# Linear attention's level products one level behind their decays and tied behind projections, and both directions' keys transposed ahead of their products

## The chip, the cores and the metric

The kernel runs on one core of one Trainium2 chip. The metric is the device time of one execution in microseconds (us). The time of the kernel before is the median of three runs.

The core has five engines that work side by side, each through its own list of instructions in order: TensorE (PE, matrix products; PEld is its weight load), VectorE (DVE), ScalarE (ACT), GpSimd (POOL) and SyncE (SP, which issues most transfers). An instruction that waits holds back everything behind it on its own engine.

## What is computed

One inference step of a two-layer network over 640 tokens (512 latent, 128 context), width 1024, all in float32. The first layer has neighbourhood attention heads beside four heads of bidirectional gated linear attention. The second has grouped-query attention. Both layers end in a gated convolutional feed-forward block. The change concerns the gated linear attention alone:

```python
def gla_scan(q, k, v, g, s0):
    # S_t = diag(alpha_t) S_{t-1} + k_t^T v_t, o_t = q_t S_t, g = log alpha <= 0
    ...
    def step(s, inp):
        qc, kc, vc, gc = inp
        bcum = jnp.cumsum(gc.astype(jnp.float32), axis=2)
        o_inter = jnp.einsum('bhid,bhde->bhie', qc * jnp.exp(bcum).astype(qc.dtype), s)
        diff = bcum[:, :, :, None, :] - bcum[:, :, None, :, :]
        decay = jnp.exp(jnp.where(causal[:, :, None], diff, -jnp.inf)).astype(qc.dtype)
        att = jnp.einsum('bhid,bhjd,bhijd->bhij', qc, kc, decay)
        o = o_inter + jnp.einsum('bhij,bhje->bhie', att, vc)
        blast = bcum[:, :, -1:, :]
        k_dec = kc * jnp.exp(blast - bcum).astype(kc.dtype)
        s_new = (jnp.exp(blast[:, :, 0, :])[..., None].astype(s.dtype) * s
                 + jnp.einsum('bhjd,bhje->bhde', k_dec, vc)).astype(s.dtype)
        return s_new, o

def gla_bidir(q, k, v, g_f, g_b, s0_f, s0_b):
    o_f, s_f = gla_scan(q, k, v, g_f, s0_f)
    flip = lambda a: jnp.flip(a, axis=2)
    o_b, s_b = gla_scan(flip(q), flip(k), flip(v), flip(g_b), s0_b)
    return o_f + flip(o_b), s_f, s_b
```

## The kernel before, in words

The activations lie with channels on the 128 partitions and the 640 tokens along the free axis, in two halves of 320 (`HN`). A float32 matrix product is done as three products of rounded parts: the weight is split into `wh` (ScalarE, line 111) and `wl` (VectorE, or GpSimd every second time in this layer, line 112), the activation into `hh` and `hl`. `step` (line 149) issues the three matmuls of one k-step into `mm`; `tokens_major` (line 578) does the same with tokens on the partitions, into `tm`, and copies each finished tile of 128 tokens to `v` (ScalarE for even tiles, VectorE for odd ones, lines 598 to 601). Its tiles take turns in two PSUM banks, so a tile needs the copy of the tile two before it.

`layer0` works on the linear attention in two pairs of heads, m = 0 and 1, in the order of the table `ORDER`: scores of pair 0 (`a0`), states of pair 0 (`s0`), scores of pair 1 (`a1`), outputs of pair 0 (`o0`), then `s1` and `o1`.

- `gla_scores` (line 834) builds the attention of each 128-token tile from levels. `level(h)` gives the decayed keys `ea` and queries `eb` for blocks of h tokens: differences of the running sums `cum` on VectorE (lines 852, 853), exponentials on ScalarE (line 832), times the keys on GpSimd (line 858) and times the queries on VectorE (line 859). Each of the six levels 0, 1, 2, 4, 8, 16 then has 40 small products `lev` on TensorE (line 872); VectorE masks their result (line 877) and GpSimd adds it up (line 879). Levels 32 and 64 come last; their products `off`/`offx` (lines 894, 898) are copied to `att` by ScalarE and VectorE (lines 903 to 908).
- `gla_states` (line 914) transposes the decayed keys `kd` on TensorE (`kdt`, line 933), copies them to `kt` on ScalarE (line 935) and multiplies them with the values (`ds`, line 940), one direction after the other. VectorE updates the states `S` (lines 945, 946).
- `gla_out` (line 951) puts `att`, `S` and the decayed queries `qd` together (`go`).

Between these pieces other work is fed in by a `Fill` (line 239), a queue of generators: first the values' projection `g_vg`, then four gate projections `rg`, then the projection `g_va` of the neighbourhood heads' values, and after `q0` the query and key projections `qk`. `fill.some(n, m)` takes n of its steps (6 `tm` or 3 `mm` matmuls each) and m steps of a side list, the modulation vectors of later layers: two VectorE instructions per step and 256 KB of weights from SyncE (lines 313, 316). The rates are constants: `RLEV` 7 and `SLEV` 2 after each level, `ROFF` 12 and `SOFF` 4 before `off`, `RST` 8 after each direction in `gla_states`, `ROUT` 6.

The order on each engine is not the program's. The kernel is built with a planner that runs through the program by priorities on an estimated timeline and puts each engine's instructions in the order that results. `tc.high_priority` shifts priorities, and `tc.issue_after(ins)` makes the instructions of its block that are on the engine of `ins` stand behind `ins`:

```python
            with tc.issue_after(ins):
                return r0.out, norm.rstd((1,), NV[1])[0]
```

Of the kernel before, what the change touches and what calls it, by code (L numbers as in the profile page):

```python
# [30 lines left out]
def kernel(ctx: ExitStack, tc: tile.TileContext, a: dict, o: dict):  # L31
# [29 lines left out]
    def P1(name, tag="p1"):  # L61
        return ps1.tile([P, 512], F32, tag=tag, name=name, bufs=2 if tag == "p1" else 1)
# [85 lines left out]

    def step(ps, w, k, hh, hl, h, start, stop):
        whi, wlo = w(k)  # L150
        s = slice(h * HN, h * HN + HN)
        for (x, y, st, sp_) in ((wlo, hh, start, False), (whi, hl, False, False), (whi, hh, False, stop)):
            nc.tensor.matmul(ps, x, y[:, s], start=st, stop=sp_)  # L153
# [85 lines left out]
    class Fill:  # L239


        def __init__(self):
            self.queue, self.aside, self.owed, self.after = [], [], 0.0, None
# [7 lines left out]
        def some(self, n, m=0):  # L251
# [326 lines left out]
    def tokens_major(src, n, H, vs, tag, bufs=None, out=None):  # L578
# [5 lines left out]
        for c in range(n // 256):  # L584
            ws = [weights(src[c, q], 1024, 256) for q in range(2)]
            for t in range(5):
                ps = P1("tm", ("mm", "po")[t % 2])[:, 0:256]
                s = slice(128 * t, 128 * t + 128)
                for k in range(KD):
# [4 lines left out]
                    nc.tensor.matmul(ps, hh[:, s], whi, start=False, stop=(k == KD - 1))  # L594
# [239 lines left out]
    def gla_scores(m, k, q, FG, fill):  # L834
# [29 lines left out]
        for li, h in enumerate(LEVELS):  # L864
            A, B = (k, q) if h == 0 else level(h)
            ps = PS("lev")
            for t in range(5):
                for e in range(2):
                    pe = slice(64 * e, 64 * e + 64)
                    for j in range(4):  # L870
                        s = slice(128 * t + 32 * j, 128 * t + 32 * j + 32)
                        nc.tensor.matmul(ps[32 * j:32 * j + 32, e, 32 * t:32 * t + 32], A[pe, s], B[pe, s], start=True, stop=True)
# [15 lines left out]
        for width in (32, 64):  # L888
            for e, pe, t, dst in blocks:
                if width == 32:  # L890
                    for j in range(4):
                        b = j // 2
                        s = slice(128 * t + 32 * j, 128 * t + 32 * j + 32)
                        nc.tensor.matmul(dst[32 * j:32 * j + 32, 64 * b:64 * b + 64], A32[pe, s],
                                         B32[pe, 128 * t + 64 * b:128 * t + 64 * b + 64], start=True, stop=True)
                    continue
                for b in range(2):
                    nc.tensor.matmul(dst[64 * b:64 * b + 64, 64 - 64 * b:128 - 64 * b],
                                     A64[pe, 128 * t + 64 * b:128 * t + 64 * b + 64],
                                     B64[pe, 128 * t + 64 - 64 * b:128 * t + 128 - 64 * b], start=True, stop=True)  # L900
# [13 lines left out]
    def gla_states(m, k, FG, vg, S, fill):  # L914
# [14 lines left out]
        for d in range(2):  # L929
            tiles = (0, 1, 2, 4) if d == 0 else (3, 2, 1, 4)  # L930
            pt = P1("kdt")
            for i, t in enumerate(tiles):
                nc.tensor.transpose(pt[:, 128 * i:128 * i + 128], kd[d][:, 128 * t:128 * t + 128], ident)
            kt = T("kt", "v2", n=512)
            nc.scalar.copy(kt[:, 0:512], pt)
            ds = P1("ds")
            for i, t in enumerate(tiles):
                for e, pe in col_pairs():
                    h = 2 * m + e
                    nc.tensor.matmul(ds[pe, 128 * i:128 * i + 128], kt[:, 128 * i + 64 * e:128 * i + 64 * e + 64],  # L940
                                     vg[t][:, 128 * h:128 * h + 128], start=True, stop=True)
# [7 lines left out]
            fill.some(RST)  # L949
# [675 lines left out]
```

## Time and profile before

| what | value |
|---|---|
| time, median of 3 runs (lowest to highest) | 1727.22 us (1725.24 to 1729.24) |
| time of the profiled execution | 1725.67 us |
| its span, first to last instruction | 1723.9 us |
| mean granted TensorE clock, share of full | 0.975 |
| busy, share of the span: PE, DVE, ACT, POOL | 95%, 73%, 43%, 12% |
| DMA | 175.22 MB, mean 102 GB/s |

A busy share is the part of the span in which an engine executes something. It is a mean over stages with different limits, so a stage is read by the table of windows, which gives busy time per engine in a stretch, and by what each engine waited for in it. Times in rows count from the first instruction of the span. A releaser (`<-DVE eb L859`) is the instruction that ended a wait last.

### The profile page before, as it was taken

The page shows a single profiled execution, that of the slowest core. Times are in us where ns is not written, and L with a number is a line of the kernel's source. Part 1 is how long each engine was busy: PE and PEld are TensorE (multiplying, and loading weights), DVE is VectorE, ACT ScalarE, POOL GpSimd, SP SyncE. Part 2 cuts the span into 40 slices and gives each one's busy share as a digit, 9 for nine tenths or more (in the row PEclk, how much of TensorE's full clock was granted, in tenths as well). Part 3 has the DMA queues.
Part 4 walks back from the last instruction along what each step waited for, and adds up shares of the span by engine and source line. Part 5 has one row for each costly group of instructions (what it writes and reads, how often), then busy time and mean ns, then how long its engine had stood idle before and what let it go on. Part 6 is the DMA issues. An engine that isn't in the chain of part 4 may idle for free.

```text
span 1723.9 us, 33442 instructions
## 1 busy us (share of the span) xinstructions
PE 1633.0 (95%) x13142; PEld 1560.4 (91%) x13142; DVE 1255.2 (73%) x2767; ACT 741.9 (43%) x1681; POOL 205.5 (12%) x473
## 2 busy tenths in 40 slices
PE   7969698999999999999999999999999999999997
PEld 6868687879999999999998888888999999999997
DVE  5899944875899989996656987885776544663664
ACT  4443254453533323322335676775453322331342
POOL 2235441310200000000003310100100000000001
PEclk8999899999999999999998999999999999999999
DMA  8623323332254455454232200120222222222222
GB/s 318 210 88 134 102 81 106 91 93 98 84 167 160 147 164 185 153 151 132 70 120 82 76 21 14 43 63 24 76 74 75 73 74 74 75 76 83 73 68 69
DMA packets 68014, 175.22 MB, mean 102 GB/s; under 512 B 7920, under 2 KB 9744, under 8 KB 66832
## 3 DMA queue, kind: packets, MB, share of 16 engines
q1 hardware_dynamic: 67024, 171.48, 30.7%
q8 instruction: 103, 1.69, 0.4%
q0 software_dynamic: 832, 1.60, 0.3%
q14 instruction: 55, 0.45, 0.1%
HBM read 165.71 MB, written 7.34 MB: 100 GB/s over the span
## 4 chain that ended last, share of the span: by engine, by line
PE 78%; DVE 13%; DMA 3%; ACT 2%; issue 2%; SPq 1%; POOL 0%; ACTq 0%; DVEq 0%; POOLq 0%
PE mm L153 66%; PE gpo L1310 2%; DVE wa L316 2%; DVE junk L316 2%; PE gpt L1298 1%; DMA wa<-in_ada_wt_dram 1%; PE gs L1289 1%; DVE wl L112 1%; PE gs L1290 1%; DVE mx L1036 1%; PE napo L1102 1%; PE ss L410 1%; DVE eb L853 1%; DMA bias<-in_na_bias_dram 1%; DVE eb L859 1%
## 5 line engine op out<-in xcount | busy, mean ns | idle before, releaser
L153 PE MATMUL mm<-hh,wl 128*128 128x320 f32 x2080 | 651.0, 315 | 9.2 <-DVE wl L112 4.1
L153 PE MATMUL mm<-hl,wh 128*128 128x320 f32 x2080 | 647.7, 312 | 0.4 <-DVE hl L456 0.4
L153 PE MATMUL mm<-hh,wh 128*128 128x320 f32 x2080 | 641.3, 311 | 0.0
L111 ACT CAST wh<-ws 128x512 fp32r<-128x512 f32 x376 | 228.5, 614 | 435.3 <-PE mm L153 401.9
L153 PEld LDWEIGHTS mm<-hh,wl 128*128 128x128 f32 x2080 | 394.0, 190 | 19.2 <-issue 9.0
L153 PEld LDWEIGHTS mm<-hl,wh 128*128 128x128 f32 x2080 | 395.1, 190 | 2.7 <-DVE h L445 1.2
L153 PEld LDWEIGHTS mm<-hh,wh 128*128 128x128 f32 x2080 | 393.5, 190 | 0.6 <-issue 0.2
L112 DVE TENSOR_TENSOR wl<-ws,wh 128x512 fp32r<-128x512 f32 x348 | 239.1, 689 | 146.5 <-ACT wh L111 145.3
L153 PE MATMUL mm<-glo,wh 128*128 128x320 f32 x704 | 217.7, 310 | 0.0
L153 PE MATMUL mm<-ghi,wh 128*128 128x320 f32 x704 | 217.7, 310 | 0.0
L153 PE MATMUL mm<-ghi,wl 128*128 128x320 f32 x704 | 215.8, 310 | 0.0
L488 DVE SCALAR_TENSOR_TENSOR x<-mm,mod,x 128x192 f32<-128x192 f32 (+2 forms) x240 | 96.9, 435 | 88.9 <-PE mm L153 88.0
L153 PEld LDWEIGHTS mm<-ghi,wl 128*128 128x128 f32 x704 | 132.3, 189 | 1.3 <-issue 1.3
L153 PEld LDWEIGHTS mm<-glo,wh 128*128 128x128 f32 x704 | 133.0, 189 | 0.0
L153 PEld LDWEIGHTS mm<-ghi,wh 128*128 128x128 f32 x704 | 132.8, 189 | 0.1
L316 DVE SCALAR_TENSOR_TENSOR junk<-wa,sb 128x512 f32<-128x512 f32 x160 | 116.9, 734 | 6.7 <-DMA wa<-in_ada_wt_dram 6.4
L316 DVE SCALAR_TENSOR_TENSOR wa<-wa,sb 128x512 f32<-128x512 f32 x160 | 118.2, 745 | 0.3
L522 POOL MEMSET u<- 128x1 f32 x88 | 8.5, 98 | 761.1 <-DVE gate L515 426.6
L525 ACT COPY u<-mm 128x320 f32<-128x320 f32 x88 | 37.7, 431 | 87.8 <-PE mm L153 82.1
L592 PE MATMUL tm<-wl,hh 128*128 128x256 f32 x200 | 58.9, 300 | 7.4 <-ACT v L601 4.4
L1042 ACT ACTIVATE gp<-gs,mx,rq 128x640 f32<-128x640 f32 x64 | 57.0, 891 | 17.3 <-DVE mx L1038 11.6
L528 ACT COPY u<-mm 128x192 f32<-128x192 f32 x88 | 28.4, 323 | 79.8 <-PE mm L153 79.8
(302 smaller groups left out, 2432.5 us busy)
## 6 DMA issues: line engine op xcount, KB each, us to landing
ws<-in_wu_dram SPq DMA_DIRECT2D x88, 512.0 KB, 3.5
wa<-in_ada_wt_dram SPq DMA_DIRECT2D x160, 256.0 KB, 3.1
ws<-in_wd_dram SPq DMA_DIRECT2D x32, 448.0 KB, 3.8
aw<-in_ada_w_dram SPq DMA_DIRECT2D x8, 1024.0 KB, 14.2
ws<-in_w_ab_dram SPq DMA_DIRECT2D x16, 512.0 KB, 10.5
ws<-in_wd_dram SPq DMA_DIRECT2D x16, 512.0 KB, 3.6
x<-in_xT_dram SPq DMA_DIRECT2D x16, 320.0 KB, 4.5
ws<-in_w_gqa_dram SPq DMA_DIRECT2D x10, 512.0 KB, 3.5
```

The source lines that it names most:

```text
L111: nc.scalar.copy(hi, src)
L112: eng.tensor_tensor(lo, src, hi, ALU.subtract)
L153: nc.tensor.matmul(ps, x, y[:, s], start=st, stop=sp_)
L316: nc.vector.scalar_tensor_tensor(w if v else junk, w, 1.0, cs[v, j], ALU.mult, ALU.mult, accum_out=acc[:, k, v, j:j + 1])
L410: nc.tensor.matmul(ps[0:rows, c:c + 2], part[:, t], onesd, start=True, stop=True)
L488: nc.vector.scalar_tensor_tensor(x[:, b:e], ps[:, b - HN * h:e - HN * h], gate[:, v, m:m + 1], old[:, b:e], ALU.mult, ALU.add)
L525: nc.scalar.copy(u[:, 1:321], ps)
L528: nc.scalar.copy(u[:, 321:513], ps[:, 0:192])
L592: nc.tensor.matmul(ps, hh[:, s], wlo, start=(k == 0), stop=False)
L853: nc.vector.tensor_tensor(v(eb), sides(NT, h, 1), sides(g, f, 0), ALU.subtract)
L1042: nc.scalar.activation(dst, src, AF.Exp, bias=mx[:, i:i + 1], accum_out=sm[:, i:i + 1], **kw)
L1310: last = nc.tensor.matmul(po[64 * f:64 * f + 64, 0:128], vs[t][:, 64 * kv:64 * kv + 64], mates[f]["x"][:, 128 * t:128 * t + 128], start=(t ...
```

## The change

Four things are changed in the first layer.

1. In `gla_scores` the products of a level are issued after the decays of the next level, so products run one level behind. Level 16's products come after the decays of level 32, and a further `fill.some(RLEV)` of seven steps follows them.
2. The products of the levels and the `off` products are tied: on TensorE they stand behind the newest matmul that the filling queue had issued by then (`fill.behind()`).
3. In `gla_states` both directions' keys are transposed and copied before the first direction's products. Four steps of the queue (`RST / 2`) follow each transposition and four each direction's products, where eight had followed each direction.
4. The transposes and the states' products are tied in the same way.

```diff
     def step(ps, w, k, hh, hl, h, start, stop):
...
-            nc.tensor.matmul(ps, x, y[:, s], start=st, stop=sp_)
+            newest[0] = nc.tensor.matmul(ps, x, y[:, s], start=st, stop=sp_).ins
...
+        def behind(self):
+
+            tie = ExitStack()
+            if self.newest is not None:
+                tie.enter_context(tc.issue_after(self.newest))
+            return tie
...
                 else:
                     n -= 1
+                    self.newest = newest[0]
...
-        for li, h in enumerate(LEVELS):
-            A, B = (k, q) if h == 0 else level(h)
+        def products(li, A, B):
             ps = PS("lev")
-            for t in range(5):
...
+            with fill.behind():
+                for t in range(5):
...
+        ready = None
+        for li, h in enumerate(LEVELS):
+            sides = (li, k, q) if h == 0 else (li, *level(h))
+            if ready:
+                products(*ready)
+            ready = sides
             fill.some(RLEV, SLEV)
         A32, B32 = level(32)
+        products(*ready)
+        fill.some(RLEV)
         A64, B64 = level(64)
         fill.some(ROFF, SOFF)
...
-        for width in (32, 64):
+        with fill.behind():
+            for width in (32, 64):
...
-        for d in range(2):
-            tiles = (0, 1, 2, 4) if d == 0 else (3, 2, 1, 4)
+        order = [(0, 1, 2, 4), (3, 2, 1, 4)]
+        kts = []
+        for d, tiles in enumerate(order):
             pt = P1("kdt")
-            for i, t in enumerate(tiles):
-                nc.tensor.transpose(pt[:, 128 * i:128 * i + 128], kd[d][:, 128 * t:128 * t + 128], ident)
+            with fill.behind():
+                for i, t in enumerate(tiles):
+                    nc.tensor.transpose(pt[:, 128 * i:128 * i + 128], kd[d][:, 128 * t:128 * t + 128], ident)
             kt = T("kt", "v2", n=512)
             nc.scalar.copy(kt[:, 0:512], pt)
-            ds = P1("ds")
...
+            kts.append(kt)
+            fill.some(RST / 2)
+        for d, tiles in enumerate(order):
+            kt, ds = kts[d], P1("ds")
+            with fill.behind():
...
-            fill.some(RST)
+            fill.some(RST / 2)
```

The planner then orders every engine of this layer anew. Behind this layer the same kinds of work follow one another as before. Three places show what moved.

TensorE, where the `off` products of the second pair of heads begin. `tm` are matmuls of the value projection `g_va`, `mm` those of the next projection. Before:

```order
L593 MATMUL tm<-wh,hl 128x256
L594 MATMUL tm<-wh,hh 128x256
L894 MATMUL off<-eb,ea 32x64
L592 MATMUL tm<-wl,hh 128x256
L894 MATMUL off<-eb,ea 32x64
L593 MATMUL tm<-wh,hl 128x256
L894 MATMUL off<-eb,ea 32x64
L594 MATMUL tm<-wh,hh 128x256
L894 MATMUL off<-eb,ea 32x64
```

and now:

```order
L603 MATMUL tm<-wh,hl 128x256
L604 MATMUL tm<-wh,hh 128x256
L915 MATMUL off<-eb,ea 32x64 x16
L915 MATMUL offx<-eb,ea 32x64 x4
L915 MATMUL off<-eb,ea 32x64 x16
L915 MATMUL offx<-eb,ea 32x64 x4
L155 MATMUL mm<-hh,wl 128x320
L155 MATMUL mm<-hl,wh 128x320
L155 MATMUL mm<-hh,wh 128x320
```

Before, the products are strewn among the last `tm` matmuls: of the 480 `tm` of both value projections 54 stand behind the first `off` row, and 75 behind the sixth `lev` block of this pair. Now none stands behind the first `off` row, and 24 behind the sixth block.

ScalarE, where the keys of the first pair are copied (`kt`); `eb` and `ea` are exponentials of the second pair's levels. Before:

```order
L111 CAST wh<-ws 128x512
L935 COPY kt<-kdt 128x512
L679 COPY rg<-mm 128x320
L111 CAST wh<-ws 128x512
L832 ACTIVATE eb<-eb 128x640
L832 ACTIVATE ea<-ea 128x640
L832 ACTIVATE eb<-eb 128x640
L935 COPY kt<-kdt 128x512
L601 COPY v<-tm 128x256
```

and now:

```order
L842 ACTIVATE eb<-eb 128x640
L111 CAST wh<-ws 128x512
L689 COPY rg<-mm 128x320
L111 CAST wh<-ws 128x512
L958 COPY kt<-kdt 128x512 x2
L611 COPY v<-tm 128x256 x2
L842 ACTIVATE ea<-ea 128x640
L842 ACTIVATE eb<-eb 128x640
```

The second copy stood behind three exponentials and now stands beside the first, with one of them ahead.

VectorE, in the last levels of the second pair; `cum` rows are the differences, `eb<-eb,kqg` the multiplications by the queries, `acc` the masked products. Before:

```order
L877 TENSOR_TENSOR acc<-lev,mask_112 128x320
L852 TENSOR_TENSOR ea<-cum 128x640
L853 TENSOR_TENSOR eb<-cum 128x640
L112 TENSOR_TENSOR wl<-ws,wh 128x512
L877 TENSOR_TENSOR acc<-lev,mask_112 128x320
L852 TENSOR_TENSOR ea<-cum 128x640
L853 TENSOR_TENSOR eb<-cum 128x640
L859 TENSOR_TENSOR eb<-eb,kqg 128x640 x2
```

and now:

```order
L887 TENSOR_TENSOR acc<-lev,mask_112 128x320
L862 TENSOR_TENSOR ea<-cum 128x640
L863 TENSOR_TENSOR eb<-cum 128x640
L336 SCALAR_TENSOR_TENSOR A_5196<-mod_1987,normg 128x16
L869 TENSOR_TENSOR eb<-eb,kqg 128x640
L887 TENSOR_TENSOR acc<-lev,mask_112 128x320
L862 TENSOR_TENSOR ea<-cum 128x640
L863 TENSOR_TENSOR eb<-cum 128x640
L869 TENSOR_TENSOR eb<-eb,kqg 128x640
L609 COPY v<-tm 128x256
```

The same kinds of instructions follow one another. Up to the last multiplication of this pair there are 96 modulation instructions, 26 differences, 14 multiplications and 12 masks in both orders; a `wl` and a `v` copy that stood behind it now stand ahead of it.

## Rows read from the trace of the kernel before

**Rows 1.** The page: the span, and VectorE, TensorE and clock in 40 slices.

```profile
span 1723.9 us, 33442 instructions
...
PE   7969698999999999999999999999999999999997
...
DVE  5899944875899989996656987885776544663664
...
PEclk8999899999999999999998999999999999999999
```

**Rows 2.** Windows: us, busy PE, PEld, DVE, ACT, POOL, then PEclk, DMA share, GB/s.

```profile
80.00:120.00 40.00, 33.78 (x315) 31.18 (x314) 39.08 (x78) 21.57 (x39) 8.21 (x4) 0.96 0.37 125
120.00:160.00 40.00, 29.23 (x643) 26.94 (x641) 40.00 (x68) 11.76 (x21) 20.81 (x13) 0.87 0.33 115
160.00:200.00 40.00, 29.86 (x446) 27.67 (x443) 39.01 (x85) 14.00 (x32) 13.71 (x9) 0.87 0.33 112
200.00:219.00 19.00, 13.98 (x321) 13.29 (x319) 17.87 (x25) 7.08 (x12) 14.33 (x10) 0.82 0.23 75
219.00:240.00 21.00, 21.00 (x247) 18.85 (x248) 4.56 (x11) 9.59 (x24) 8.27 (x7) 1.00 0.33 108
```

**Rows 3.** TensorE's waits from 96 to 231 us: total, times, longest.

```profile
PE lev L872 <- DVE eb L859: 8.6, 4, 5.0
PE ds L940 <- ACT kt L935: 7.2, 1, 7.2
...
PE mm L153 <- DVE wl L112: 4.1, 1, 4.1
PE tm L592 <- DVE v L599: 2.3, 1, 2.3
PE lev L872 <- DVE acc L877: 2.3, 1, 2.3
...
PE off L894 <- DVE eb L859: 1.4, 1, 1.4
```

**Rows 4.** VectorE's groups by form, 96 to 231 us: busy, mean ns, idle before.

```profile
L316 DVE SCALAR_TENSOR_TENSOR wa<-wa,sb 128x512 f32<-128x512 f32 x27 | 25.7, 964 | 0.1
L316 DVE SCALAR_TENSOR_TENSOR junk<-wa,sb 128x512 f32<-128x512 f32 x27 | 25.0, 935 | 0.8 <-DMA wa<-in_ada_wt_dram 0.7
L859 DVE TENSOR_TENSOR eb<-eb,kqg 128x640 f32<-128x640 f32 x14 | 17.5, 1268 | 0.5 <-ACT eb L832 0.5
```

**Rows 5.** ScalarE's and TensorE's timelines at the second key copy: start, us, instruction, idle before.

```profile
180.96 0.74 ACT L832 ACTIVATE eb<-eb 128x640 f32<-128x640 f32 x1 [9.94 <-DVE eb L853]
...
183.07 0.57 ACT L935 COPY kt<-kdt 128x512 f32<-128x512 f32 x1
...
183.69 1.97 PE L940 MATMUL ds<-v,kt 128*64 128x128 f32 x16 [7.18 <-ACT kt L935]
```

**Rows 6.** VectorE's timeline at the end of the second pair's scores.

```profile
215.22 0.49 DVE L877 TENSOR_TENSOR acc<-lev,mask 128x320 f32<-128x320 f32 x1 [0.59 <-PE lev L872]
...
218.72 1.24 DVE L859 TENSOR_TENSOR eb<-eb,kqg 128x640 f32<-128x640 f32 x1 [0.53 <-ACT eb L832]
226.31 0.42 DVE L599 COPY v<-tm 128x256 f32<-128x256 f32 x1 [6.35 <-PE tm L594]
227.07 0.69 DVE L112 TENSOR_TENSOR wl<-ws,wh 128x512 fp32r<-128x512 f32 x1 [0.34 <-ACT wh L111]
231.75 2.60 DVE L907 COPY att<-acc 32x160 f32<-32x160 f32 x8 [3.98 <-ACT att L904]
```

**Rows 7.** TensorE's timeline at the same place.

```profile
214.03 1.08 PE L872 MATMUL lev<-eb,ea 64*32 64x32 f32 x80 [5.02 <-DVE eb L859]
...
229.26 0.68 PE L898 MATMUL off<-eb,ea 64*64 64x64 f32 x18
...
230.40 0.41 PE L153 MATMUL mm<-hh,wl 128*128 128x320 f32 x1
```

**Rows 8.** Windows of the `tm` tile alone: columns as in rows 2, without POOL.

```profile
215.00:219.10 4.10, 4.05 (x21) 3.85 (x21) 0.41 (x1) 0.00 (x0) 0.63 0.03 8
222.60:228.50 5.90, 5.90 (x48) 5.69 (x48) 0.42 (x1) 0.14 (x1) 1.00 0.25 92
```

**Rows 9.** VectorE's and GpSimd's timelines: multiplications beside GpSimd's, and one alone.

```profile
120.44 5.79 DVE L859 TENSOR_TENSOR eb<-eb,kqg 128x640 f32<-128x640 f32 x3
...
120.03 1.89 POOL L858 TENSOR_TENSOR ea<-ea,kqg 128x640 f32<-128x640 f32 x1 [2.76 <-ACT ea L832]
...
199.20 0.81 DVE L859 TENSOR_TENSOR eb<-eb,kqg 128x640 f32<-128x640 f32 x1
```

**Rows 10.** ScalarE's and TensorE's timelines at the second pair's keys.

```profile
247.68 0.59 ACT L935 COPY kt<-kdt 128x512 f32<-128x512 f32 x1
248.16 0.64 ACT L111 CAST wh<-ws 128x512 fp32r<-128x512 f32 x1
...
248.33 0.88 PE L940 MATMUL ds<-v,kt 128*64 128x128 f32 x12 [0.35 <-ACT kt L935]
```

**Rows 11.** Timelines of VectorE, TensorE and SyncE's queue, first units of neighbourhood attention.

```profile
268.98 0.69 DVE L1075 TENSOR_TENSOR nas<-nas,bias 128x512 f32<-128x512 f32 x1
...
269.74 12.99 SPq L1064 DMA_DIRECT2D bias<-in_na_bias_dram  x3
...
281.68 0.70 DVE L1075 TENSOR_TENSOR nas<-nas,bias 128x512 f32<-128x512 f32 x1 [7.21 <-DMA bias<-in_na_bias_dram]
...
285.87 1.51 PE L1083 MATMUL napt<-ident,nap 128*128 128x128 f32 x6 [6.36 <-DVE nap L1050]
```

More of the change, by code (lines that the diff above doesn't have):

```diff
@@ L147, in weights @@
         return part
+    newest = [None]
     def step(ps, w, k, hh, hl, h, start, stop):
@@ L242, in __init__ @@
         def __init__(self):
-            self.queue, self.aside, self.owed, self.after = [], [], 0.0, None
+            self.queue, self.aside, self.owed, self.after, self.newest = [], [], 0.0, None, None
+        def behind(self):
[3 more added lines that the diff above has]
+            return tie
         def add(self, gen):
@@ L593, in tokens_major @@
                     nc.tensor.matmul(ps, hl[:, s], whi, start=False, stop=False)
-                    nc.tensor.matmul(ps, hh[:, s], whi, start=False, stop=(k == KD - 1))
+                    newest[0] = nc.tensor.matmul(ps, hh[:, s], whi, start=False, stop=(k == KD - 1)).ins
                     if k % 2:
@@ L863, in gla_scores @@
         acc, tmp = accs[:, 0:320], accs[:, 320:640]
-        for li, h in enumerate(LEVELS):
-            A, B = (k, q) if h == 0 else level(h)
+        def products(li, A, B):
             ps = PS("lev")
-            for t in range(5):
[L868 to L872, printed above, removed]
+            with fill.behind():
+                for t in range(5):
+                    for e in range(2):
+                        pe = slice(64 * e, 64 * e + 64)
+                        for j in range(4):
+                            s = slice(128 * t + 32 * j, 128 * t + 32 * j + 32)
+                            nc.tensor.matmul(ps[32 * j:32 * j + 32, e, 32 * t:32 * t + 32], A[pe, s], B[pe, s], start=True, stop=True)
             pv = ps[:, :, 0:160].rearrange("p e (t i) -> p e t i", i=32)
@@ L887, in gla_scores @@
                   for e in range(2) for t in range(5)]
-        for width in (32, 64):
[L889 to L900, printed above, removed]
+        with fill.behind():
+            for width in (32, 64):
+                for e, pe, t, dst in blocks:
+                    if width == 32:
+                        for j in range(4):
+                            b = j // 2
+                            s = slice(128 * t + 32 * j, 128 * t + 32 * j + 32)
+                            nc.tensor.matmul(dst[32 * j:32 * j + 32, 64 * b:64 * b + 64], A32[pe, s],
+                                             B32[pe, 128 * t + 64 * b:128 * t + 64 * b + 64], start=True, stop=True)
+                        continue
+                    for b in range(2):
+                        nc.tensor.matmul(dst[64 * b:64 * b + 64, 64 - 64 * b:128 - 64 * b],
+                                         A64[pe, 128 * t + 64 * b:128 * t + 64 * b + 64],
+                                         B64[pe, 128 * t + 64 - 64 * b:128 * t + 128 - 64 * b], start=True, stop=True)
         for e in range(2):
```

10 lines of the change are left out of this document (5 added, 5 removed).

## The prediction
> **What bounds the kernel now.** I read the page's 40 slices first. TensorE is nearly always full; it dips in slices 3 and 5 (86 to 129 and 172 to 215 us), where VectorE is at nine tenths from slice 3 to 5 and the clock sags in slice 5 [rows 1]. So the windows of that stretch come next [rows 2]. In the linear attention, from 80 to 219 us, VectorE is busy 39.08, 40.00 and 39.01 us of 40 and 17.87 of 19: it is full. TensorE works 33.78, 29.23, 29.86 and 13.98 us, 106.9 of 139 together, at granted clocks of 0.82 to 0.96. From 219 to 240 us it is the other way round: TensorE 21.00 of 21.00, VectorE 4.56. Before 219 us, then, VectorE sets the time, and after it TensorE.
>
> The waits say what TensorE lacks there [rows 3]: levels wait for VectorE's multiplications (8.6 us in four waits) and masks (2.3), the states for their second key copy (7.2), projections for VectorE's `wl` and `v` (4.1 and 2.3), `off` for the last multiplication (1.4). These six make 25.9 us. Only part of them has an edit behind it, and none shortens VectorE's list, half of whose time in this stretch is work the change leaves alone, as 54 modulation instructions of 25.7 + 25.0 us [rows 4].
>
> The place that counts is the hand-over. VectorE's fourteenth multiplication of this stretch, that of level 64 of the second pair, starts at 218.72 us and takes 1.24, so it ends at 219.96 [rows 6]. The last `off` products need nothing else that is late, yet they end at 230.40, where the next `mm` begins [rows 7]. In between TensorE runs `tm` matmuls, 48 of them in 5.90 us, 0.123 us each [rows 8], while VectorE idles 6.35 us [rows 6]. TensorE had waited for VectorE earlier, and now pays the work that would have fitted there.
>
> **The change, part by part.**
>
> *Products one level behind, and tied.* The work of no engine grows by it: the same 480 `tm`, the same products. The order says what moves: behind the first `off` stood 54 `tm`, now none; behind the sixth `lev` block of this pair 75, now 24. They go into time in which TensorE waits. Room is there: it has 139 - 106.9 = 32.1 us without work in [rows 2], and 54 x 0.123 = 6.6 us are to fit.
>
> So the end of the `off` products comes from VectorE's list. Ahead of the fourteenth multiplication stand the same modulations, differences, multiplications and masks as before, and besides one `v` copy (0.42 us) and one `wl` (0.69) that stood behind it [rows 6]: 219.96 + 1.11 = 221.07 us. After it come the 64-wide products, 229.26 to 230.40, 1.14 us [rows 7]: 222.21. That is 230.40 - 222.21 = **8.2 us earlier**. TensorE's own list gives about the same by another way: 75 - 24 = 51 `tm` fewer behind the sixth block are 6.3 us, and 21 of them ran in 4.10 us at a clock of 0.63 after an idle of 5.02 us [rows 7, 8], where 21 x 0.123 = 2.6 would do; those 1.5 us go as well if that idle goes. Sum 7.8. I take 8.2.
>
> The outputs `go` wait for the copies of `att`, the last of which ends at 231.75 + 2.60 = 234.35, 3.95 us after the `off` products [rows 6, 7]. Projection matmuls covered that before. In the new order some of them stand ahead of the last `off`; the same 408 stand ahead of the first `go` in all, so a short idle may open there, but the first `go` still moves by the whole 8.2. If the clock falls after that idle, it costs about what it cost before: 1.5 us [rows 8].
>
> What I hold fixed is VectorE's speed. Three multiplications took 5.79 us beside GpSimd's product of 1.89, and one alone took 0.81 [rows 9]; the mean of 14 is 1.27 [rows 4]. At 1.27 - 0.81 = 0.46 each, the last five, whose neighbours the new order shuffles most, can move the milestone by 2.3 us either way; I take zero, since as many of both are issued. The Trainium skill speaks against taking it so (SBUF — State Buffer, Who interferes with whom): a VectorE instruction with two SBUF inputs and a GpSimd one that reads SBUF share a port pair, and issue order decides who blocks. The 5.79 us agree with a block; by that rule a new order could take all 14 x 0.46 = 6.4 us or add as much, and the sum below, -7.2 by the row, would be anything from -13.6 to -0.8.
>
> *The further `fill.some` of seven steps* adds no work. It draws the queue's matmuls forward past level 64, and is part of the 54.
>
> *Keys ahead, first pair.* Now the second copy stands behind three exponentials, whose inputs ScalarE awaits from VectorE (9.94 us), and TensorE loses 7.18 [rows 5]. With both copies together this wait goes. It frees TensorE, not VectorE, and is worth nothing of its own: it is room for the `tm` above. Next in line is VectorE's `v` copy, which a `tm` tile needs from the tile two before it; it stands behind the state updates. I expect TensorE to be held there 5 to 9 us, that is for about what the key wait leaves. The bound below is nothing, the bound above the 7.18 itself, if VectorE were not full; then the rival below holds.
>
> *Keys ahead, second pair.* Here TensorE is full, so a wait costs. The `kt` copy ended at 248.27 and the products began at 248.33 after an idle of 0.35 [rows 10]. Now both copies stand behind one more `wh` cast (0.64), and both (0.59 each) ahead of the first product, so it is ready 0.64 + 0.59 = 1.2 us later; part of it is covered by projections. I take **+1.0**. Below it may be 0, above 3, if both transposes wait in turn for PSUM as well.
>
> *Behind it.* The neighbourhood attention has an idle of 6.36 us on TensorE, since a bias transfer is late: VectorE waits 7.21 us for it [rows 11]. Its issue, at 269.74, follows the addition at 268.98 + 0.70 = 269.68, which frees its buffer. So it moves with the work, and the idle stays: zero, with -6.4 (lands in time) and +7 (stays where it is, the idle takes all of the gain) as bounds.
>
> The sum is -8.2 + 1.0 = **-7.2 us** on the profiled execution: 1725.67 - 7.2 = 1718.5. That execution lies 1.55 us under the median 1727.22; against the median it is **1720.0**. A difference under 0.2%, 3.5 us, can hardly be told from none.
>
> **The rivals.**
>
> *All gaps count.* If VectorE is full only because its waits are hidden in its order, every wait of [rows 3] that has an edit behind it comes off: -25.9 at most, 1701.3 us. For it speaks that TensorE is the bound of the kernel, against it 39 to 40 us of 40 on VectorE over 80 us [rows 2], with 0.8 us of idle at the modulations [rows 4]. The Trainium skill would have one look here first (Perfetto Trace Analysis, Optimization Strategy): find the gaps on the engine one optimizes and make what they wait for come sooner. It also says that the most contended engine changes between regimes; by [rows 2] it is VectorE here, so the 25.9 are no price. 0.05.
>
> *The gain is given back.* The bias lands at 281.68 whatever comes before, or the copies of `att` and `kt` hold what was won. Then TensorE's idle of 6.36 becomes some 13, and the time stays within 0.2%: about 1727. For it: transfers have their own queue, and the bias took from 269.74 to 281.68, far longer than its position in the queue asks. Against it: its issue hangs on the work. 0.23.
>
> *VectorE waits for the products: slower.* A tied block stands behind all `tm` issued before it. The order has 30 to 36 `tm` there, 36 x 0.123 = 4.4 us, and TensorE itself is held by `v`. VectorE has no slack: if it reaches its mask `acc` before the block is done, its idle goes on the path whole. Before, the one such wait at the end was 0.59 us [rows 6]. If five blocks of the second pair come 2 us late each, that is +10, net +2.8: 1730.0; if each is 4.4 late, +22, net +14.8. It decides from the point at which TensorE reaches a block later than VectorE its mask. Against it: products are one level late, so VectorE has a whole level's differences and multiplication to do first, several us. 0.15.
>
> *The bias lands in time.* -7.2 - 6.4 = -13.6: 1713.6. 0.07.
>
> **How the numbers follow.** The forecast has 0.50. Its own range takes the 2.3 us of the ports, 0 to 3 for the second pair and 1.5 for the clock: -10.5 to -1.4 against the median, 1716.7 to 1725.8. Below it lies the bias case (0.07), above it the gain given back (0.23). From 1712 to 1729 us the range holds these and leaves out the 0.05 of all gaps and most of the 0.15 of the slower rival. Faster by over 0.2%: 0.50 + 0.07 + 0.05 = 0.62; same 0.23; slower 0.15.
>
> **What would show it.** Right: VectorE still at 39 to 40 us of 40 from 80 to 200 us; the wait of 7.18 us for `kt` gone; no `tm` among the `off` products, and the 6.35 us of VectorE for `tm` gone; the `off` products end near 222 us, the first `go` about 8 us earlier than before. Wrong: VectorE's masks show idle time ended by `lev` (the slower rival), the idle before `napt` grows from 6.36 towards 13 (given back), or VectorE's share from 120 to 200 us drops with an earlier end (all gaps).

## The result, and the profile after

The changed kernel takes 1718.02 us (median of 6 runs, 1713.76 to 1721.09) against 1729.32 us for the kernel before beside it (6 runs, 1725.24 to 1735.22). The ratio on record is 0.9931 (the quotient of the medians would be 0.9935), with a 95% interval of 0.9908 to 0.9955: 11.3 us, or 0.7%, faster. Forecast were 1720.0 us and a range of 1712 to 1729; against the median 1727.22 that the forecast was added to, it is 9.2 us faster where 7.2 were expected. So the forecast of the time held. Of its terms the largest came out smaller, and one that had been put at zero came out at 4.3 us; more on this in the account below.

The page of the changed kernel, the lines that answer to [rows 1]:

```profile
span 1717.3 us, 33434 instructions
...
PE   7997898999999999999999999999999999999997
...
DVE  5899955775999999996657987885866544663664
...
PEclk8997899999999999999999999999999999999998
```

TensorE's dip in slice 3 is gone (6 became 9) and the one in slice 5 is smaller (6 became 8). Slice 4 has a new one (9 became 7), and the clock sags there now. The windows by stage (columns as in rows 2), before:

```profile
0.00:80.00 80.00, 68.99 (x491) 58.66 (x492) 57.10 (x156) 33.61 (x73) 18.22 (x25) 0.91 0.73 265
80.00:219.00 139.00, 106.84 (x1713) 99.08 (x1711) 135.96 (x252) 54.41 (x102) 57.06 (x36) 0.89 0.33 111
219.00:260.00 41.00, 39.36 (x428) 35.38 (x428) 15.76 (x31) 22.86 (x49) 16.64 (x15) 1.00 0.29 94
260.00:400.00 140.00, 124.84 (x1004) 109.40 (x1004) 90.76 (x189) 69.23 (x185) 26.29 (x30) 0.95 0.30 90
400.00:1700.00 1300.00, 1279.86 (x9418) 1246.06 (x9418) 945.77 (x2112) 556.24 (x1263) 81.70 (x353) 0.99 0.29 92
```

and after:

```profile
0.00:80.00 80.00, 68.40 (x488) 57.96 (x489) 56.20 (x153) 33.93 (x73) 18.15 (x25) 0.89 0.73 265
80.00:219.00 139.00, 115.69 (x1751) 107.93 (x1750) 132.93 (x250) 53.20 (x101) 55.62 (x34) 0.86 0.35 115
219.00:260.00 41.00, 37.54 (x412) 34.92 (x412) 19.56 (x32) 25.04 (x53) 20.04 (x16) 0.92 0.37 116
260.00:400.00 140.00, 128.26 (x1016) 111.98 (x1015) 94.14 (x196) 69.11 (x182) 26.75 (x42) 0.96 0.27 82
400.00:1700.00 1300.00, 1280.49 (x9440) 1247.57 (x9439) 944.55 (x2114) 556.26 (x1265) 82.43 (x352) 0.99 0.29 92
```

Read the first column minus TensorE's: the time in which TensorE had nothing to run. In the scores and first states (80 to 219 us) it falls from 32.2 to 23.3 us. In the second states and outputs (219 to 260) it rises from 1.6 to 3.5, in the neighbourhood attention (260 to 400) it falls from 15.2 to 11.7, and behind 400 us it is 20.1 and 19.5. Each kernel was profiled a second time (below): there the same stretches have 29.7 and 24.0, 1.6 and 3.8, 16.9 and 11.7, 19.2 and 19.9. In the mean of two profiles that is -7.3, +2.0, -4.3 and +0.1 us, and +0.9 in the first 80 us: 8.6 us less idle time together. The windows are cut at fixed times, not at the same work: the changed kernel's wait of 1.06 us before `off`, shown below, belongs to the scores but lies behind 219 us.

Idle time saved is not yet time won. The two pairs of profiled executions differ by 6.6 us (1725.67 and 1719.05) and 4.5 us (1725.78 and 1721.24) only, since TensorE was busy 3.9 and 2.2 us longer in the changed kernel, at a mean granted clock of 0.972 in place of 0.975 and 0.974. Near the end of the neighbourhood attention the changed kernel was 3.1 us ahead, and 3.8 in the second pair; the other 3.5 and 0.7 us came behind it, where TensorE's idle time is the same. TensorE, the last `ctxo` products (the context's) there, before and then after:

```profile
399.20 0.44 PE L1145 MATMUL ctxo<-ctxx,v 128*64 128x128 f32 x4
```

```profile
396.09 0.44 PE L1172 MATMUL ctxo<-ctxx,v 128*64 128x128 f32 x4
```

In the medians the clock goes the other way: it was 0.9719 in the mean over 73 runs of the kernel before, taken beside the experiments on four chips, and 0.9745 over the changed kernel's six runs. A straight line through the 73 runs falls by 0.7 us for each 0.001 of the clock, so by estimate that difference is worth about 2 us, near the 2.7 that are missing between 8.6 and 11.3. No run isolates it.

TensorE's waits from 80 to 226 us, after:

```profile
PE tm L602 <- DVE v L609: 6.3, 2, 3.2
PE lev L882 <- DVE eb L869: 4.0, 3, 1.5
PE tm L602 <- ACT v L611: 3.4, 2, 2.4
PE lev L882 <- DVE mod L330: 3.4, 1, 3.4
```

The 8.6 us for the multiplications became 4.0 (7.3 and 6.1 in the second profiles), and the 7.2 for the key copy are gone [rows 3]; the `v` copy on VectorE is the costliest now. The end of the second pair's scores, VectorE and GpSimd, then TensorE, to be held against [rows 6, 7]:

```profile
221.36 2.04 DVE L112 TENSOR_TENSOR wl<-ws,wh 128x512 fp32r<-128x512 f32 x1
223.32 1.90 DVE L869 TENSOR_TENSOR eb<-eb,kqg 128x640 f32<-128x640 f32 x1
...
220.87 1.98 POOL L868 TENSOR_TENSOR ea<-ea,kqg 128x640 f32<-128x640 f32 x1
```

```profile
225.38 0.68 PE L919 MATMUL off<-eb,ea 64*64 64x64 f32 x18 [1.06 <-DVE eb L869]
...
226.51 0.42 PE L155 MATMUL mm<-hl,wh 128*128 128x320 f32 x1
...
228.68 0.49 PE L992 MATMUL go<-att,v 128*128 128x128 f32 x3
```

The last multiplication ends at 225.22, later than the 219.96 before, but TensorE now stands ready for it: `off` ends at 226.5 in place of 230.4, and the first `go` starts at 228.7 in place of 234.0 (TensorE, before):

```profile
234.03 2.39 PE L965 MATMUL go<-att,v 128*128 128x128 f32 x20
```

VectorE's wait of 6.35 us for `tm` is gone.

Of the signs that were named for a right forecast, the wait of 7.18 us for `kt`, the `tm` among the `off` products and VectorE's 6.35 us went as they should. Three others were missed: `off` ended at 226.5 and not near 222; the first `go` came 5.4 us earlier (4.4 in the second pair of profiles) and not about 8; and VectorE was busy 36.3 us of 40 from 160 to 200 us, not 39 to 40.

### The profile page after: what moved, and what is told of

Same layout as the page of the kernel before. It is cut to its first block, busy times and chain, and to the rows that moved or that the text cites. A ratio compares the mean times of both kernels' runs of the same rounds, so it can differ in the third digit from the quotient of the medians.

```text
span 1717.3 us, 33434 instructions
## 1 busy us (share of the span) xinstructions
PE 1636.9 (95%) x13142; PEld 1565.8 (91%) x13142; DVE 1255.1 (73%) x2767; ACT 741.8 (43%) x1681; POOL 206.5 (12%) x473
## 3 DMA queue, kind: packets, MB, share of 16 engines
q8 instruction: 103, 1.69, 0.4%
## 4 chain that ended last, share of the span: by engine, by line
PE 78%; DVE 13%; ACT 3%; DMA 3%; issue 2%; POOL 0%; SPq 0%; ACTq 0%; DVEq 0%; POOLq 0%
PE mm L155 67%; PE gpo L1337 2%; DVE junk L326 2%; DVE wa L326 2%; DMA wa<-in_ada_wt_dram 2%; PE gpt L1325 1%; DVE wl L112 1%; PE gs L1316 1%; PE gs L1317 1%; DVE eb L863 1%; PE ss L420 1%; PE napo L1129 1%; DVE mx L1063 1%; DVE ea L862 1%; DVE eb L869 1%
## 5 line engine op out<-in xcount | busy, mean ns | idle before, releaser
L326 DVE SCALAR_TENSOR_TENSOR wa<-wa,sb 128x512 f32<-128x512 f32 x160 | 113.8, 718 | 0.3
L1069 ACT ACTIVATE gp<-gs,mx,rq 128x640 f32<-128x640 f32 x64 | 57.0, 891 | 16.2 <-DVE mx L1065 11.3
```

Of the source, the lines that this page charges most:

```text
L326: nc.vector.scalar_tensor_tensor(w if v else junk, w, 1.0, cs[v, j], ALU.mult, ALU.mult, accum_out=acc[:, k, v, j:j + 1])
L1069: nc.scalar.activation(dst, src, AF.Exp, bias=mx[:, i:i + 1], accum_out=sm[:, i:i + 1], **kw)
```

## The experiments

All are set beside runs of the kernel before on the same chip. The chips differ from one group of experiments to the next, so what is compared below is the gain over those runs, and not one median with another. "Idle" is TensorE's, by the windows above; the whole change has 23.3 and 24.0, 3.5 and 3.8, 11.7 and 11.7 in its two profiles.

| kernel | median us | ratio to before, 95% interval | idle 80-219 | idle 219-260 | idle 260-400 | mean clock |
|---|---|---|---|---|---|---|
| whole change | 1718.02 | 0.9931 (0.9908 to 0.9955) | 23.3 | 3.5 | 11.7 | 0.9745 |
| products alone | 1728.84 | 0.9991 (0.9982 to 1.0000) | 26.0 | 4.5 | 14.7 | 0.9734 |
| states alone | 1726.50 | 0.9984 (0.9973 to 0.9995) | 30.9 | 0.4 | 14.0 | 0.9733 |
| without ties | 1717.65 | 0.9936 (0.9917 to 0.9955) | 23.4 | 3.7 | 12.0 | 0.9763 |
| without the further steps | 1722.93 | 0.9960 (0.9946 to 0.9975) | 25.8 | 4.5 | 10.8 | 0.9732 |
| 30 modulations behind | 1734.62 | 1.0031 (1.0020 to 1.0043) | 14.8 | 21.9 | 15.3 | 0.9677 |
| VectorE +7 differences | 1726.11 | 0.9979 (0.9969 to 0.9989) | 26.3 | 5.3 | 11.7 | 0.9719 |
| 12 modulations behind | 1718.03 | 0.9934 (0.9918 to 0.9950) | 17.9 | 8.2 | 10.4 | 0.9727 |
| 18 modulations behind | 1728.79 | 1.0001 (0.9991 to 1.0010) | 16.6 | 14.1 | 13.8 | 0.9702 |
| 12 behind, kc first | 1723.79 | 0.9971 (0.9958 to 0.9983) | 17.0 | 7.4 | 14.0 | 0.9718 |
| 8 behind, kc first | 1716.63 | 0.9925 (0.9911 to 0.9939) | 21.0 | 5.2 | 11.4 | 0.9756 |

**The two halves.** After the first profile two theories stood against each other: the hand-over of the forecast, and one on transfers, since the idle of 6.36 us before `napt` [rows 11] was gone and SyncE's queue had changed.

Products alone (the states as before):

```diff
-        order = [(0, 1, 2, 4), (3, 2, 1, 4)]
-        kts = []
-        for d, tiles in enumerate(order):
+        for d in range(2):
+            tiles = (0, 1, 2, 4) if d == 0 else (3, 2, 1, 4)
...
-            fill.some(RST / 2)
+            fill.some(RST)
```

> The scores as changed (products one level behind and tied, the further seven steps), the states as in the kernel before. On SyncE's queue all eight loads of vw again stand behind a ws load, as before; with the whole change three of them stand ahead of it. Hand-over theory (the gain is that no tm is left behind the last levels): the off products end at 226 to 227 us and the time falls by 6 to 10 us, as with the whole change. Transfer theory (the gain is that vw, ws and so the bias land earlier, which the states' part brings): the idle of 6.4 us before napt stays and the time falls by 0 to 3 us.

States alone (the scores as before):

```diff
-        def products(li, A, B):
-            ps = PS("lev")
-            with fill.behind():
+        for li, h in enumerate(LEVELS):
+            A, B = (k, q) if h == 0 else level(h)
+            ps = PS("lev")
...
-        products(*ready)
-        fill.some(RLEV)
```

> The states as changed (both keys transposed ahead, tied), the scores as before. On SyncE's queue four loads of vw stand ahead of the ws load that held them before. Hand-over theory: the 7.2 us wait for kt goes, but VectorE is full there, so the off products still end near 230 us and the time stays within 2 us of before. Transfer theory: the bias is on time, the idle of 6.4 us before napt is gone, and the time falls by 4 to 8 us. If every wait of TensorE counted: -7 us from the key copy alone.

Neither half does it: 0.5 and 2.8 us off the medians of the runs beside them (1729.34), 3.3 together where the whole gives 11.3. With the products alone the time is what the transfer theory expected, while `off` ended at 226.1 us, as the hand-over theory said, and 4.9 us of idle time went from the scores (26.0 against 30.9, the mean of the two profiles before). It came back elsewhere: 2.9 us from 219 to 260, 1.3 in the first 80 us and 1.8 behind 400. There this wait appeared in the second layer, on whose instructions there is no edit, but which the planner had put in another order (waits of TensorE, 945 to 1200 us; the kernel before has 0.4 there, and one of 2.0 for a `v` copy that is gone here):

```profile
PE gs L1310 <- ACT gp L1063: 4.6, 2, 4.2
```

With the states alone the wait for the second key copy is gone, and this stands in its place (TensorE, then ScalarE):

```profile
189.10 1.09 PE L882 MATMUL lev<-eb,kqg 64*32 64x32 f32 x80 [10.66 <-DVE eb L869]
```

```profile
181.44 0.74 ACT L842 ACTIVATE eb<-eb 128x640 f32<-128x640 f32 x1 [10.10 <-DVE eb L863]
```

10.66 us for VectorE where 7.18 us for the copy were [rows 5], so the idle time of the scores stays at 30.9. That half's gain lies behind: idle 0.4 from 219 to 260, 14.0 from 260 to 400, the latter 2.0 below the mean of before. The transfer theory is right on its fact and wrong on the price: the bias was on time, and the kernel gained 2.8 us where 4 to 8 were expected.

**Without the ties** (`behind()` returns an empty tie):

```diff
-            if self.newest is not None:
+            if False:
                 tie.enter_context(tc.issue_after(self.newest))
```

> The whole change without the four ties. The order still has no tm behind the last off products of the second pair and three vw loads ahead of the ws load; only small blocks of the levels move ahead of some tm. Both theories: the time of the whole change within 2 us, since neither the hand-over nor the loads differ. If the ties themselves bring the gain: 4 to 8 us slower than the whole change.

1717.65 us, a gain of 11.7: the ties are worth nothing that can be measured.

**Without the further steps:**

```diff
         products(*ready)
-        fill.some(RLEV)
         A64, B64 = level(64)
```

> The whole change without the further seven steps of the queue after level 16's products. 54 tm then stand between the last block of levels and the off products of the second pair instead of 24. Hand-over theory: if TensorE has to run those 30 tm after VectorE's last multiplication it is 30 x 0.12 = 3.6 us slower than the whole change; if it runs them while VectorE works on levels 32 and 64, the same time within 1 us. Transfer theory: four vw loads ahead of the ws load, so the same time as the whole change.

The gain is 6.4 us in place of 11.3; the intervals of the two ratios overlap a little, so the loss of some 5 us is likely rather than shown. The reason given for one did not hold. `off` ended at 225.7 us, no later than with the whole change, so TensorE ran the 30 `tm` under VectorE's last levels. VectorE's last multiplication had even ended 2.0 us earlier, at 223.2: in this order the `wl` stands behind it, and not ahead of it. The idle time is in the scores ahead of that, 25.8 us, in `tm` tiles that wait for the `v` copies (TensorE, 80 to 226 us):

```profile
PE tm L602 <- DVE v L609: 8.0, 3, 6.0
PE tm L602 <- ACT v L611: 5.0, 4, 3.3
```

**Does VectorE set the end of the scores?** Two kernels ask it from both sides. Modulations out of the stretch:

```diff
                     fill.until(g_vg)
-                    fill.some(0, 99)
                     gla_states(m, kg[m], cum[m], vg, S, fill)
...
                 piece(p[0], int(p[1]))
+        fill.some(0, 99)
         fill.until(g_va)
```

> The whole change, with the rest of the modulation steps drawn after the second pair's outputs instead of ahead of the first pair's states. Ahead of VectorE's fourteenth multiplication stand 66 modulation instructions in place of 96: 30 x 0.95 = 28 us less. If VectorE sets the end of the scores: that multiplication ends 10 to 28 us earlier than the 225.2 of the whole change, TensorE's idle time from 160 to 219 us (10.3 us with the whole change) falls below 4, and the time falls by up to 8 us more than with the whole change, less what the 30 instructions cost in front of the second pair's state updates. If VectorE's list does not set the end: the same idle time and the same time within 2 us, or slower since the states then wait for the modulations.

and more work for it:

```diff
             nc.vector.tensor_tensor(v(eb), sides(NT, h, 1), sides(g, f, 0), ALU.subtract)
+            if m == 1:
+                nc.vector.tensor_tensor(v(eb), sides(NT, h, 1), sides(g, f, 0), ALU.subtract)
```

> The whole change with the eb difference of each of the second pair's seven levels issued twice (the second writes the same values again): 7 x 1.33 = 9.3 us more on VectorE. If VectorE sets the end of the scores: the fourteenth multiplication ends 7 to 10 us later than 225.2, and the time rises by 6 to 10 us over the whole change. If the products or TensorE set it: less than 2 us.

It does. With more work the last multiplication ended at 236.66, 11.4 us later (7 to 10 were expected), and the gain over the kernel before fell from 11.3 to 3.9 us (VectorE):

```profile
235.83 0.83 DVE L871 TENSOR_TENSOR eb<-eb,kqg 128x640 f32<-128x640 f32 x1 [0.86 <-ACT eb L842]
```

With 30 instructions fewer ahead of it, it ended at 213.5 us, 11.7 us earlier (VectorE):

```profile
211.58 1.90 DVE L869 TENSOR_TENSOR eb<-eb,kqg 128x640 f32<-128x640 f32 x1
```

TensorE's idle time in the scores fell to 14.8 us, and from 160 to 219 us to 1.2: there it had become the bound itself. Yet the kernel was slower than before, by this (TensorE):

```profile
264.85 0.76 PE L995 MATMUL go<-qd,S 64*128 64x128 f32 x2 [24.18 <-DVE S L972]
```

The moved modulations stood between the `att` copies and the state updates, and some waited for their weights up to 4.3 us:

```profile
220.43 2.04 DVE L326 SCALAR_TENSOR_TENSOR junk<-wa,sb 128x512 f32<-128x512 f32 x1
...
228.87 0.68 DVE L326 SCALAR_TENSOR_TENSOR junk<-wa,sb 128x512 f32<-128x512 f32 x1
...
250.52 0.69 DVE L326 SCALAR_TENSOR_TENSOR junk<-wa,sb 128x512 f32<-128x512 f32 x1 [4.29 <-DMA wa<-in_ada_wt_dram]
```

**Profiles again.** Both kernels once more, unchanged.

> The kernel before once more, for a second profile. If the difference between before and after lies in TensorE's idle time, and the clock only scatters: idle time over the span within 1.5 us of the first profile's 80, and the clock's loss (32 there) free to differ by several us. If the clock carries the difference: the idle time is no steadier than the clock.

> The changed kernel once more, for a second profile. Idle theory: TensorE's idle time again 69 to 71 us, the clock's loss different from the 37 of the first profile. Clock theory: both move alike.

The waits listed on TensorE add up to 79.9 and 77.7 us before, 69.2 and 71.1 after; span less busy time gives 90.9 and 88.8, 80.4 and 82.0. So the idle time repeats within some 2 us (a little wider than expected) and tells the kernels apart. The spans, 1723.9 and 1724.0, 1717.3 and 1719.5, don't show the clock to scatter more than that; the six runs of the changed kernel, from 1713.76 to 1721.09, scatter more than its idle time.

**Some modulations behind.** If VectorE has too much up to 219 us and little behind it, part of the list could be moved:

```diff
-                    fill.some(0, 99)
+                    fill.some(0, 9 if m == 0 else 0)
...
                 piece(p[0], int(p[1]))
+        fill.some(0, 99)
         fill.until(g_va)
```

> The whole change, with nine modulation steps drawn ahead of the first pair's states and the last ones behind the second pair's outputs: 84 modulation instructions ahead of the fourteenth multiplication in place of 96, and 12 between it and the second pair's first state update, 12 x 0.7 to 2 us of VectorE's 21 us that are free there. If VectorE sets the end of the scores: that multiplication ends about 11 us earlier than 225.2 (no earlier than the 213.5 at which TensorE had no more to wait for), TensorE's idle time from 160 to 219 us falls from 10.3 below 5, the states don't wait for the modulations, and the time falls by 4 to 8 us below the whole change. If moved modulations always land in front of something that TensorE needs: no gain, the idle time comes back at the go products.

> The same with six steps: 78 modulation instructions ahead, 18 behind. If VectorE's free time from the att copies to the states (about 15 us) holds 18 instructions as well as 12: the time of the other within 2 us. If they outlast it (18 x 1 us, and their transfers): 3 to 6 us slower than with 12, with a wait of go for S.

With 12 behind, the idle time of the scores fell by 5.4 us to 17.9, but `ds` waited longer (TensorE, then ScalarE):

```profile
244.76 1.55 PE L968 MATMUL ds<-v,kt 128*64 128x128 f32 x12 [4.62 <-ACT kt L959]
```

```profile
242.05 0.62 ACT L111 CAST kch<-kc 128x512 fp32r<-128x512 f32 x1 [3.12 <-DMA kc<-in_na_kc_dram]
```

A cast in front of the `kt` copies waited for a load that now stood behind the modulations' weights on SyncE's queue. The gain was given back: 1718.03 us, or 11.4 us off, as with the whole change. With 18 behind it was worse, 1728.79 us. The wait of `go` for `S` that had been expected was 1.1 us; the same cast waited 14.1 us for its load, and TensorE 10.5 us for ScalarE behind it. So the loads of `kc` were drawn first, by moving the last draw behind them:

```diff
-        fill.some(0, 99)
         fill.until(g_va)
...
             kcl.append(y.rearrange("p (h t) -> p h t", h=4))
+        fill.some(0, 99)
```

> As with 12 modulation instructions behind, but their steps are drawn after the loads of kc (the neighbourhood attention's context keys), so that on SyncE's queue the kc loads stand ahead of the wa loads, where they stood with the whole change. With 12 behind, ScalarE's kch cast waited 3.1 us for kc in front of the kt copies, and TensorE 4.6 us for kt. If that transfer order was what gave the gain back: the wait of ds for kt is below 1.5 us, and the time falls 3 to 5 us below the whole change, to 1713 to 1715. If another wait takes its place (S behind a modulation, the vw loads behind wa): the same time as the whole change within 2 us.

> The same with eleven steps: 88 modulation instructions ahead of the fourteenth multiplication, 8 behind. If VectorE's list sets the end of the scores: 4 x 0.95 = 4 us later there than with 12 behind, still 8 us earlier than with the whole change; the time 1 to 3 us above that with 12, and 1 to 4 us below the whole change.

The wait for `kt` fell to 0.87 us as expected, but with 12 behind another took its place. VectorE stood 10.28 us at a modulation whose weights now came behind the `vw` loads, with `kl` behind it in its list, and TensorE waited 5.48 us for the keys (VectorE, then TensorE):

```profile
258.43 1.35 DVE L326 SCALAR_TENSOR_TENSOR junk<-wa,sb 128x512 f32<-128x512 f32 x1 [10.28 <-DMA wa<-in_ada_wt_dram]
```

```profile
262.75 0.55 PE L1099 MATMUL nas<-kk,q 128*128 128x256 f32 x1 [5.48 <-ACT kk L708]
```

1723.79 us, a gain of 5.5. With 8 behind it is 1716.63 us (5 runs), the fastest median of the study; its ratio to before of 0.9925 (0.9911 to 0.9939) overlaps that of the whole change, so it isn't shown to be better. Its profile was 7 to 8 us ahead of the whole change's two at the last `ctxo` product of this layer (start 387.99), and lost 2 to 6 us of that again behind 400 us, at the same idle time; the reason stays open.

## Why the prediction was right, and where its working was not

**That VectorE sets the end of the scores** held, and is shown from both sides (11.7 us earlier, 11.4 later). The point that followed from it held too, that the key copies of the first pair are worth nothing of their own: the states alone turned 7.18 us of wait into 10.66. The `v` copy that was named as late next costs 6.3 us, inside the 5 to 9 forecast.

**The size of the hand-over was off.** Forecast were an end of `off` at 222.2 us and 8.2 us of gain. By the end of its last row it ended at 226.6 and 228.4 in the two profiles, 230.5 and 231.4 before: 3.9 and 3.0 us. The step that failed is "219.96 + 1.11 = 221.07", which lets VectorE reach its last multiplication with the two added instructions and no new wait. The multiplication ended 4.1 us after that, at 225.22. VectorE's windows from 96 us to the end of that multiplication (columns as in rows 2), before and then after, and its groups from 96 to 226 us after, show where the time went:

```profile
96.00:219.96 123.96, 91.91 (x1553) 85.90 (x1544) 121.84 (x208) 44.13 (x89) 57.34 (x36) 0.88 0.31 105
```

```profile
96.00:225.22 129.22, 105.00 (x1758) 98.95 (x1756) 123.75 (x210) 46.09 (x94) 61.21 (x38) 0.87 0.33 105
```

```profile
L326 DVE SCALAR_TENSOR_TENSOR junk<-wa,sb 128x512 f32<-128x512 f32 x27 | 26.5, 991 | 3.6 <-DMA wa<-in_ada_wt_dram 3.5
L326 DVE SCALAR_TENSOR_TENSOR wa<-wa,sb 128x512 f32<-128x512 f32 x27 | 21.5, 809 | 0.0
...
L869 DVE TENSOR_TENSOR eb<-eb,kqg 128x640 f32<-128x640 f32 x14 | 16.0, 1146 | 1.7 <-ACT eb L842 1.7
```

It idled 5.5 us where it had idled 2.1, 3.4 us more (2.7 more in the second pair of profiles): 3.6 us for weights that came later and 1.7 for exponentials, where these two had been 0.8 and 0.5 [rows 4]. It was busy 1.9 us longer, where 1.1 had been counted: the `wl` costed at 0.69 us took 2.04 beside GpSimd, and other groups became shorter. The cross-check by TensorE's list agreed with the 8.2 because it counted the same `tm`, not because it was independent of VectorE. In idle time what came was closer to it: 7.3 us less in the scores, 6.2 if the wait before `off` that lies behind 219 us is counted with them. Part of that is the earlier end; part is ten matmuls of the next projection that now run ahead of the last `off` products, from 222.6 to 224.3 us; and part went into a lower clock, 0.86 from 80 to 219 us against 0.89 in the first pair of profiles, 0.85 against 0.86 in the second.

**The second pair's keys** were to cost 1.0 us, with bounds of 0 and 3. Idle time from 219 to 260 us rose by 2.0, of which 1.1 is the wait before `off`; the 0.9 that are left agree with the number, but not with its working. The key copy cost 0.35 us more (0.5 in the second pair), and the wait for a copy of the first outputs, which projections had covered before, 1.4; a wait of 1.0 us for `kl` is gone from this stretch (TensorE):

```profile
242.46 1.38 PE L992 MATMUL go<-att,v 128*128 128x128 f32 x10 [1.69 <-ACT got L999]
245.12 1.12 PE L967 MATMUL ds<-v,kt 128*64 128x128 f32 x8 [0.70 <-ACT kt L958]
```

**The neighbourhood attention** was put at zero, since the bias would move with the work. It gave 4.3 us: the rival in which the bias lands in time came true beside the forecast. The step that failed is that only the issue of the bias mattered. After, the bias was issued at 271.06, 1.3 us later than before, and yet no addition waited for it. SyncE's waits for a transfer already under way, before and then after (220 to 300 us):

```profile
SPq L1064 <- DMA bias<-in_na_bias_dram: 10.6, 1, 10.6
```

```profile
SPq L1091 <- DMA bias<-in_na_bias_dram: 1.8, 1, 1.8
```

Before, all eight `vw` loads stood behind a `ws` load that waited for VectorE, and the bias was caught behind them. In the new order three of the eight stand ahead of it, at 232.1 us in place of 249.6 (SyncE's queue, before and then after, 215 to 300 us):

```profile
249.55 5.52 SPq L782 DMA_DIRECT2D vw<-values  x5
```

```profile
232.10 1.84 SPq L792 DMA_DIRECT2D vw<-values  x3
...
271.06 6.65 SPq L1091 DMA_DIRECT2D bias<-in_na_bias_dram  x3
```

The states' half alone brings such an order too (four ahead), and with it the wait before `napt` went; with the products alone, which has the old order, 3.5 us of it stayed. No run moves these loads by themselves, so that their order is the cause is argued, not shown. The stretch gained 4.3 and not 6.4 us, since waits for the keys `kk` grew from 2.6 to 5.1.

**The rivals.** The slower one did not come: after, VectorE waits for `lev` not at all in one profile of the scores and 0.5 us in the other. All gaps together are not the price either: of the 25.9 us that TensorE waited in [rows 3], new waits for `v` and `rg` took the place of many. In idle time, with the wait before `off` counted to the scores, the terms came out at -6.2, +0.9 and -4.3, with +0.9 ahead of the stage, where -8.2, +1.0 and 0 were forecast. A hand-over 2.0 us too hopeful and 0.9 us that had no term stood against 4.3 the other way, and the clock, which had no term of its own in the sum, took some of it in the profiles and added some in the medians. That the time came within 2 us of the forecast is in part luck. A further rival was not tested: how much a new order by the planner gives or takes without any edit of this kind.

The Trainium skill (SBUF — State Buffer, Who interferes with whom) had been weighed and set aside: issue order decides whether VectorE or GpSimd is blocked. This case's traces agree that the same instruction can cost either: the `wl` of 2.04 us began while GpSimd's multiplication (220.87 to 222.85 us) was running, against 0.69 us before [rows 6], and the modulations of 2.04 and 0.68 us above are one instruction beside GpSimd and alone. Single groups moved by up to 4.2 us (the `wa` modulations from 25.7 to 21.5), but in both directions, so taking zero for their sum was 0.8 us off here, and the new waits cost more.

## What to carry to other kernels

When one engine is full in a stage, find the instruction of its list that the next stage waits for, and ask what the other engines still have to do after it; that work, and not the sum of their waits, was what the new order could save here. Ask as well what the new order puts in front of that instruction, and what it will have to wait for. Work that is moved out of a full stage lands in front of something: read each queue it passes, the loads' above all, since a load that comes late holds everything behind the instruction that needs it, as the 10.28 us above did. Halves of a change that is planned anew are not terms of a sum: 0.5 and 2.8 us here, 11.3 together.

## What the runs showed of the hardware that was not expected

- VectorE's modulation instruction, two inputs in SBUF, took 0.68 us alone (at 228.87 us, in the kernel with 30 modulations behind) and 2.04 us (at 220.43) while GpSimd multiplied two tiles: three times as long. GpSimd there:

```profile
219.91 3.96 POOL L947 TENSOR_TENSOR kd<-kd,kqg 128x640 f32<-128x640 f32 x2
```

- Short idle times were followed by a lower clock as well. After 2.3 us of idle time in five, the wait of 1.69 us for `got` among them, the granted clock of the changed kernel was 0.50, the lower of the two levels (1.2 GHz), over five microseconds in which TensorE was busy 4.88. In the second profile it was 0.66 from 245 to 250 us; in the kernel before, with no idle time from 240 to 245 us and 0.7 us from 245 to 250, it stayed at 1.00 (windows of the changed kernel, columns as in rows 2):

```profile
240.00:245.00 5.00, 2.73 (x18) 2.00 (x16) 2.22 (x3) 5.00 (x11) 1.45 (x2) 0.90 0.13 48
245.00:250.00 5.00, 4.88 (x37) 4.55 (x38) 3.26 (x7) 3.41 (x8) 2.25 (x3) 0.50 0.40 140
```

- An order that is planned anew reaches far: with the products alone, a new wait of 4.2 us appeared some 700 us behind the work of the last edited line.
